# Score products of both token tiles in one block, and a fixed order for TensorE inside the token mixer

## The chip, the cores and the metric

The kernel runs on one core of a Trainium2 chip. The metric is the device time of one execution in microseconds (us), taken as the median of several runs. Besides it there is one profiled execution of the kernel before, from whose trace all durations below are read.

## The reference

The kernel computes a trunk of two layers on x of 256 tokens by 1024 channels, in float32, conditioned by a vector c. Each layer is a half-step SwiGLU feed-forward block (inner width 2816), a token mixer, and another half-step feed-forward block, each of them behind an RMS norm with shift and scale. The change is in the token mixer, which is this, cut to what matters:

```
def token_mixing(n, ...):
    proj = n @ w_in                              # qa 512, ka 128, va 128, qd 512, kd 512, vd 512 columns
    qa = axial_rope(rms_norm(qa), ...)           # 8 query heads of 64
    ka = axial_rope(rms_norm(ka), ...)           # 2 key heads of 64
    ya = gqa_attention(qa, ka, va) @ w_ba        # softmax(q k^T / 8) v, 4 query heads per key head
    od = diff_attention(qd, kd, vd, lam, slopes) # 4 heads, w = softmax(s0 + bias) - lam * softmax(s1 + bias)
    od = rms_norm(od, subln_g) * (1.0 - lam_init)
    yb = od.reshape(b, s, B_WIDTH) @ w_bb
    g = jax.nn.sigmoid(n @ w_gate + b_gate)
    ga, gb = jnp.split(g, 2, axis=-1)
    return (ga * ya + gb * yb) @ w_o
```

## The kernel before

**Products.** Every float32 matrix product is made of three products of half-split operands: high by high, low by high, high by low (`mm3`, L86 to L88). A weight comes by DMA into one of four `raw` buffers of 128x1024; ACT casts it to its high half `whi` (L328), DVE subtracts to get the low half `wlo` (L330). TensorE (PE) then streams products of 128 rows by 128x256, most of them straight after one another.

**The order of the work.** The kernel's text gives one list of steps for each layer's mixer (L1024 to L1093). A scheduler takes that list and sets the order of instructions on each engine by times that it simulates for itself, so that on PE a step of the list that would have to wait is moved behind products of a later step. What was read from PSUM comes in four general banks (`gen`, taken by turns: transposes, scores, `od`, `ont`) and four accumulating banks (`acc`).

**Branch A.** `post_kv(t)` makes the rotated and normed keys `kr` of token tile t on DVE; the norm's power is taken on POOL (L124). `to_T` transposes the queries `qr` (four transposes) and the keys `kr` (one) on PE into a `tt` bank (L787); DVE subtracts the low halves `qaT`, `kaT` (L791). Between and after these stand the projections `proj_T("qd", part)` and `proj_T("kd", part)`, 48 products each into `pt` banks. `a_scores(jj, t)` makes the scores of pair jj of query heads for one token tile: 12 products whose contraction is over 64 rows, in two `gen` banks (L840). DVE takes the maxima `nmx` (L844) and ACT the exponentials `p` (L852). `a_norm` scales them, `a_T` transposes them, `a_pv` multiplies them with the values.

**Branch B.** `b_scores(pair, t)` makes 12 products of 64 rows as well (L909), into two `gen` banks that DVE reads into `xb` (L916, adding the distance penalty and taking the maximum), ACT takes the exponentials, `b_norm` makes the difference of the two maps on DVE (L933, L934), `b_T(hd)` transposes one head, `b_out(t)` multiplies with `vd` into `od`, and `b_outT(t)` scales `od` to `on` (L970), transposes it into an `ont` bank (L973) and splits it (`onf` L977, `odL` L981).

**The gate.** `gate_mm(j, half)`, 24 full products into an `acc` bank `gt`, sixteen of them per layer, stands between these steps.

During the mixer DVE and ACT also take part in the weights of the next stage: `gacc` (L276) and `raw·cb` (L245) read a raw weight of 128x1024 on DVE. The mixer of layer 0 lies at about 205 to 345 us in the trace and that of layer 1 at about 742 to 880 us.

Of the kernel before, what the change touches and what calls it, by code (L numbers as in the profile page):

```python
# [19 lines left out]
P = 128  # L20
D = 1024
S = 256
L = 2
# [19 lines left out]
def trunk(tc, a):  # L43
    nc = tc.nc
    with (
# [38 lines left out]

        def mm3(out, Lh, Ll, Rh, Rl, start, stop):
            nc.tensor.matmul(out, Lh, Rh, start=start, stop=False, skip_group_check=True)  # L86
            nc.tensor.matmul(out, Ll, Rh, start=False, stop=False, skip_group_check=True)  # L87
            nc.tensor.matmul(out, Lh, Rl, start=False, stop=stop, skip_group_check=True)  # L88
# [26 lines left out]
        for hf in range(2):  # L115
            x = slice(hf * 512, (hf + 1) * 512)
            bank = gen("cb")
            cmm = nc.tensor.matmul(bank, ones[0:1, :], crow[hf], start=True, stop=True)
            cact = nc.scalar.activation(cb[:, x], bank, AF.Silu)
# [169 lines left out]
        def gate_bcast(l, s):  # L289
# [5 lines left out]
            for hf in range(2):  # L295
# [5 lines left out]
                nc.tensor.matmul(bank, onesr, gh, start=True, stop=False, skip_group_check=True)  # L301
                nc.tensor.matmul(bank, onesr, gl, start=False, stop=True, skip_group_check=True)
# [57 lines left out]
        class Norm:  # L360
# [37 lines left out]
            def transposes(self):  # L398
                self.banks = []
                for hf in range(2):  # L400
                    bank = gen("nt")
                    for i in range(4):
                        nc.tensor.transpose(bank[:, i * P:(i + 1) * P], self.xs[hf][:, i * P:(i + 1) * P], ident)
# [89 lines left out]
        def tok_hi(bank, ncol, unit_of, nT, t):  # L493
# [4 lines left out]
            for k in range(NK):  # L498
# [3 lines left out]
                nc.tensor.matmul(bank, nh[:, k, tok], wh[:, x], start=k == 0, stop=False, skip_group_check=True)  # L502
                nc.tensor.matmul(bank, nh[:, k, tok], wl[:, x], start=False, stop=False, skip_group_check=True)

        def tok_lo(bank, ncol, unit_of, nT, t, last):
            nh, nl = nT
            tok = slice(t * P, (t + 1) * P)
            for k in range(NK):
                u, i, c = unit_of(k)
                wh, wl = half(u, i)  # L510
                nc.tensor.matmul(bank, nl[:, k, tok], wh[:, c:c + ncol], start=False, stop=k == NK - 1, skip_group_check=True)
# [37 lines left out]
        def first_T(hts):  # L549

            tb = gen("tb")
            for t in range(2):
                for c in range(2):
                    nc.tensor.transpose(tb[:, c * 256 + t * P:c * 256 + (t + 1) * P], hts[t][:, c * P:(c + 1) * P], ident)
# [6 lines left out]
        def ffn(i, nT, norm1, first, nT_next):  # L561
# [6 lines left out]
            def down_mm(idx, t, hf, last, y=slice(0, 512), part=False):  # L568
# [4 lines left out]
                for c in range(2):  # L573
                    x = slice(c * 512 + y.start, c * 512 + y.stop)
                    if part and c == 1:

                        for L, R in ((hh, wh), (hl, wh)):
                            nc.tensor.matmul(acc[t][hf], L[:, c, tok], R[:, x], start=False, stop=False, skip_group_check=True)
                        for z in (slice(0, PART), slice(PART, 512)):
                            nc.tensor.matmul(acc[t][hf][:, z], hh[:, c, tok], wl[:, 512 + z.start:512 + z.stop], start=False,  # L580
# [136 lines left out]
        def mixer(i, nT, norm1, consts, nT_next):  # L717
# [65 lines left out]
            def to_T(src, dst, t, n):  # L783

                bank = gen("tt")
                for i in range(n):
                    nc.tensor.transpose(bank[:, i * P:(i + 1) * P], src[:, i * P:(i + 1) * P], ident)  # L787
# [44 lines left out]
            def a_scores(jj, t):  # L832
# [3 lines left out]
                for i in range(2):  # L836
                    for x, y in ((0, 0), (1, 0), (0, 1)):
                        for v in range(2):
                            pr = slice(v * 64, (v + 1) * 64)
                            nc.tensor.matmul(banks[v][:, i * 256:(i + 1) * 256], st["qaT"][x][pr, 2 * jj + i, tok], kaT[y][pr, 0, :],  # L840
# [29 lines left out]
            def a_T(jj, i):  # L870
                for v in range(2):
                    bank = gen("pt")
                    for t in range(2):
                        for c in range(2):
                            nc.tensor.transpose(bank[:, c * 256 + t * P:c * 256 + (t + 1) * P],
# [5 lines left out]
            def a_pv(jj):  # L881
                ot = gen("ot")

                for i in range(2):
                    for c in range(2):
                        for v in range(2):
                            nc.tensor.matmul(ot[v * 64:(v + 1) * 64, i * 256:(i + 1) * 256], va[:, c, v * 64:(v + 1) * 64],
# [12 lines left out]
            def b_scores(pair, t):  # L900
# [3 lines left out]
                for m in range(2):  # L904
                    ch = m * 2 + pair
                    for x, y in ((0, 0), (1, 0), (0, 1)):
                        for e in range(2):
                            pr = slice(e * 64, (e + 1) * 64)
                            nc.tensor.matmul(scs[e][:, m * 256:(m + 1) * 256], st["qdT"][x][pr, ch, tok], st["kdT"][y][pr, ch, :],  # L909
# [26 lines left out]
            def b_T(hd):  # L936
                bank = gen("wt")
                for t in range(2):
                    for c in range(2):
                        nc.tensor.transpose(bank[:, c * 256 + t * P:c * 256 + (t + 1) * P], xs[hd, t][0][:, c * P:(c + 1) * P], ident)  # L940
# [7 lines left out]
            def b_out(t):  # L948
                tok = slice(t * P, (t + 1) * P)
                od = gen("od")  # L950
                for hd in range(4):
                    for c in range(2):
                        nc.tensor.matmul(od[:, hd * P:(hd + 1) * P], wTs[hd][:, c, tok], st["vd"][:, c, hd * P:(hd + 1) * P],
# [10 lines left out]
            def b_outT(t):  # L964
# [7 lines left out]
                for hd in range(4):  # L972
                    nc.tensor.transpose(bank[:, hd * P:(hd + 1) * P], on[:, hd * P:(hd + 1) * P], ident)  # L973
# [52 lines left out]
            st["qaT"] = pair("qaT")  # L1026
            to_T(st["qr"][0], st["qaT"], 0, 4)
# [7 lines left out]
            a_scores(0, 0)  # L1035
# [370 lines left out]
```

## Time and profile before

| | |
|---|---|
| median of 3 runs | 1097.06 us (1096.51 to 1097.66) |
| profiled execution, its own time | 1097.68 us |
| its span | 1095.9 us |
| granted TensorE clock, mean | 0.999 |
| PE busy | 1082.9 us, 99% of the span, 7796 instructions |
| DVE busy | 864.9 us, 79%, 1388 instructions |
| ACT busy | 593.1 us, 54%, 916 instructions |
| POOL busy | 44.5 us, 4%, 52 instructions |
| chain that ended last | PE 94% of it, DVE 3% |

The shares are averages over the whole span. PE is nearly always at work, so a change is worth what it adds to or takes from PE's own time, or what it makes PE wait; an engine that has idle time overall can still be late at one place. The profiled execution spends 1.8 us outside the span.

### The profile page before, as it was taken

To read this page: it belongs to the slowest core of one execution; us is meant where nothing else is said; L and a number is where in the kernel's file an instruction comes from. 1 tells how busy PE (TensorE), PEld (TensorE's weight loads), DVE (VectorE), ACT (ScalarE), POOL (GpSimd) and SP (SyncE) were. 2 spreads that over 40 slices of the span, in tenths; PEclk is the share of its full clock that TensorE was granted. 3 is DMA by queue.
4 is the path that set the end of the run, shared out by engine and by line. 5 is a ranking of instruction groups with operands and counts; after the bars stand their busy time and mean duration, and the time that the engine had idled before them with its cause. 6 is when DMAs were issued, how large, how long until landed. Compare 5 with 4: busy or idle time off the path is not lost.

```text
span 1095.9 us, 19235 instructions
## 1 busy us (share of the span) xinstructions
PE 1082.9 (99%) x7796; PEld 998.8 (91%) x7796; DVE 864.9 (79%) x1388; ACT 593.1 (54%) x916; POOL 44.5 (4%) x52
## 2 busy tenths in 40 slices
PE   8999999999999999999999999999999999999997
PEld 6989999898999899999989999989889998999996
DVE  5998986899978798886589886569988779766543
ACT  5564483558664554535455545435776547444432
POOL 1000000220010000000000000004000000000000
PEclk9999999999999999999999999999999999999999
DMA  8998996368745299997449987543865454876501
GB/s 315 380 368 336 380 335 219 120 263 332 264 172 193 86 376 357 347 377 266 150 152 357 365 288 285 202 165 126 297 236 189 157 190 183 315 267 229 197 19 39
DMA packets 44889, 271.12 MB, mean 247 GB/s; under 512 B 5880, under 2 KB 6648, under 8 KB 14848
## 3 DMA queue, kind: packets, MB, share of 16 engines
q1 hardware_dynamic: 42340, 267.93, 66.1%
q10 hardware_dynamic: 2460, 1.96, 0.6%
q8 instruction: 61, 1.00, 0.3%
q14 instruction: 28, 0.23, 0.1%
HBM read 268.82 MB, written 1.05 MB: 246 GB/s over the span
## 4 chain that ended last, share of the span: by engine, by line
PE 94%; DVE 3%; ACT 1%; issue 1%; POOL 0%; POOLq 0%
PE dn L87 6%; PE dn L88 6%; PE dn L86 6%; PE u L86 6%; PE g L86 6%; PE u L87 6%; PE g L88 6%; PE g L87 6%; PE u L88 6%; PE gt L86 3%; PE gt L88 3%; PE gt L87 3%; PE g L1199 2%; PE u L1199 2%; PE yb L88 1%; PE yb L87 1%
## 5 line engine op out<-in xcount | busy, mean ns | idle before, releaser
L330 DVE TENSOR_TENSOR wlo<-raw,whi 128x1024 fp32r<-128x1024 f32 x364 | 436.9, 1220 | 133.7 <-PE u L87 44.6
L328 ACT CAST whi<-raw 128x1024 fp32r<-128x1024 f32 x364 | 374.0, 1052 | 226.4 <-PE u L88 83.7
L86 PE MATMUL u<-nh,whi 128*128 128x256 f32 x592 | 164.0, 277 | 0.0
L86 PE MATMUL g<-nh,whi 128*128 128x256 f32 x592 | 164.0, 277 | 0.0
L87 PE MATMUL u<-nh,wlo 128*128 128x256 f32 x592 | 163.7, 277 | 0.0
L88 PE MATMUL g<-nl,whi 128*128 128x256 f32 x592 | 163.7, 277 | 0.0
L87 PE MATMUL g<-nh,wlo 128*128 128x256 f32 x592 | 163.7, 277 | 0.0
L88 PE MATMUL u<-nl,whi 128*128 128x256 f32 x592 | 163.6, 276 | 0.0
L86 PE MATMUL dn<-whi,hh 128*128 128x512 f32 (+1 forms) x326 | 126.0, 387 | 0.0
L87 PE MATMUL dn<-whi,hl 128*128 128x512 f32 (+1 forms) x326 | 125.9, 386 | 0.0
L88 PE MATMUL dn<-wlo,hh 128*128 128x512 f32 (+1 forms) x326 | 125.8, 386 | 0.0
L86 PEld LDWEIGHTS g<-nh,whi 128*128 128x128 f32 x592 | 111.2, 188 | 0.3
L87 PEld LDWEIGHTS g<-nh,wlo 128*128 128x128 f32 x592 | 111.2, 188 | 0.2
L86 PEld LDWEIGHTS u<-nh,whi 128*128 128x128 f32 x592 | 111.2, 188 | 0.1
L87 PEld LDWEIGHTS u<-nh,wlo 128*128 128x128 f32 x592 | 111.3, 188 | 0.0
L88 PEld LDWEIGHTS u<-nl,whi 128*128 128x128 f32 x592 | 111.2, 188 | 0.2
L88 PEld LDWEIGHTS g<-nl,whi 128*128 128x128 f32 x592 | 111.2, 188 | 0.0
L245 DVE CUSTOM_DVE_ANT_0 raw<-raw,cb 128x1024 f32<-128x1024 f32 x80 | 95.5, 1217 | 1.1 <-DMA raw<-in_ada_t_dram 0.9
L86 PE MATMUL gt<-nh,whi 128*128 128x256 f32 x256 | 73.7, 288 | 0.0
L88 PEld LDWEIGHTS dn<-wlo,hh 128*128 128x128 f32 x326 | 61.2, 188 | 12.4
L87 PEld LDWEIGHTS dn<-whi,hl 128*128 128x128 f32 x326 | 61.3, 188 | 11.1 <-DVE hl L546 0.2
L86 PEld LDWEIGHTS dn<-whi,hh 128*128 128x128 f32 x326 | 61.3, 188 | 11.1
(227 smaller groups left out, 2051.9 us busy)
## 6 DMA issues: line engine op xcount, KB each, us to landing
raw<-in_w_gu_dram SPq DMA_DIRECT2D x79, 1024.0 KB, 5.5
raw<-in_w_d_dram SPq DMA_DIRECT2D x41, 1024.0 KB, 6.4
raw<-in_ada_t_dram SPq DMA_DIRECT2D x40, 1024.0 KB, 6.8
raw<-in_ada_g_dram SPq DMA_DIRECT2D x24, 1024.0 KB, 6.3
raw<-in_w_in_dram SPq DMA_DIRECT2D x16, 1024.0 KB, 5.0
raw<-in_w_gate_dram SPq DMA_DIRECT2D x16, 1024.0 KB, 4.9
raw<-in_ada_t_dram SPq DMA_DIRECT2D x16, 512.0 KB, 6.5
raw<-in_w_gu_dram SPq DMA_DIRECT2D x32, 256.0 KB, 6.1
```

Source lines behind the costliest of these rows:

```text
L86: nc.tensor.matmul(out, Lh, Rh, start=start, stop=False, skip_group_check=True)
L87: nc.tensor.matmul(out, Ll, Rh, start=False, stop=False, skip_group_check=True)
L88: nc.tensor.matmul(out, Lh, Rl, start=False, stop=stop, skip_group_check=True)
L245: queue("dve", nc.vector.tensor_tensor_reduce(r, r, cb, 1.0, 0.0, op0=ALU.mult, op1=ALU.add, accum_out=col[:, k:k + 1]))
L328: split[1] = nc.scalar.copy(hi, r)
L330: split[0] = nc.vector.tensor_tensor(lo, r, hi.bitcast(F32), op=ALU.subtract)
L1199: nc.tensor.matmul(bank[:, c * 256:(c + 1) * 256], W[:, w], N[:, k, :], start=x + y + k + c == 0, stop=y == 1 and k == NK - 1, skip_group_ ...
```

## The change

A small class `Ordered` wraps PE's `matmul` and `transpose`. While its flag `on` is set, every PE instruction is tied behind the one issued before it (an order on the same engine, no semaphore). The flag is set from the first `to_T` of the mixer to its last `gate_mm`, in each layer. So the scheduler can no longer move PE's instructions against one another there: what the list says is what PE does, and a PE instruction that isn't ready holds all that stand behind it. The list itself is written anew: the score steps of both token tiles stand together (`a_scores(0,0)`, `a_scores(0,1)`, and so on), and so do `a_T`, `b_T` and `b_outT` of a pair.

```diff
+        class Ordered:
+            on, last = False, None
+            def then(self, ins):
+                if self.on and self.last is not None:
+                    follow(ins, self.last)
+                self.last = ins
+                return ins
+            def matmul(self, *args, **kw):
+                return self.then(nc.tensor.matmul(*args, **kw))
+            def transpose(self, *args, **kw):
+                return self.then(nc.tensor.transpose(*args, **kw))
+        pe = Ordered()
         def mm3(out, Lh, Ll, Rh, Rl, start, stop):
-            nc.tensor.matmul(out, Lh, Rh, start=start, stop=False, skip_group_check=True)
+            pe.matmul(out, Lh, Rh, start=start, stop=False, skip_group_check=True)
...
             st["qaT"] = pair("qaT")
+            pe.on = True
             to_T(st["qr"][0], st["qaT"], 0, 4)
             to_T(st["kr"][0], kaT, 0, 1)
             qd, kd = [], []
             proj_T("qd", 0, qd)
             post_kv(1, kv[1])
             to_T(st["qr"][1], st["qaT"], 1, 4)
             to_T(st["kr"][1], kaT, 1, 1)
             proj_T("qd", 1, qd)
             a_scores(0, 0)
+            a_scores(0, 1)
             proj_T("kd", 0, kd)
             a_norm(0, 0)
-            a_scores(0, 1)
+            a_norm(0, 1)
             proj_T("kd", 1, kd)
-            a_norm(0, 1)
             a_T(0, 0)
+            a_T(0, 1)
             vd0 = proj("vd", 0)
-            a_T(0, 1)
             st["vd"] = slot("vd", (P, 2, 512))
             nc.scalar.copy(st["vd"][:, 0, :], vd0)
+            a_pv(0)
+            vd1 = proj("vd", 1)
+            nc.scalar.copy(st["vd"][:, 1, :], vd1)
             a_scores(1, 0)
-            vd1 = proj("vd", 1)
-            a_norm(1, 0)
-            a_pv(0)
-            nc.scalar.copy(st["vd"][:, 1, :], vd1)
             a_scores(1, 1)
...
             gate_mm(2, 1)
+            b_scores(0, 0)
+            b_scores(0, 1)
+            gate_mm(3, 0)
+            b_norm(0, 0)
             b_norm(0, 1)
+            gate_mm(3, 1)
             b_scores(1, 0)
-            gate_mm(3, 0)
-            b_T(0)
-            gate_mm(3, 1)
-            b_T(1)
-            b_norm(1, 0)
             b_scores(1, 1)
             free(4)
             cap_w[0] = CAP2
             gate_mm(4, 0)
+            b_T(0)
+            b_T(1)
             gate_mm(4, 1)
+            b_norm(1, 0)
             b_norm(1, 1)
             gate_mm(5, 0)
+            gate_mm(5, 1)
             b_T(2)
-            gate_mm(5, 1)
             b_T(3)
+            gate_mm(6, 0)
             b_out(0)
-            gate_mm(6, 0)
             b_out(1)
             free(3)
             gate_mm(6, 1)
+            gate_mm(7, 0)
             b_outT(0)
-            gate_mm(7, 0)
             b_outT(1)
             gate_mm(7, 1)
+            pe.on = False
             gate_bcast(l, 1)
```

Nothing is added to or taken from any engine's instructions; only their order, and with it their waits, differ. In the changed file the helper lines stand 9 to 21 lines further down, and all products carry L97, all transposes L100.

On PE, at the start of the ordered part in layer 0, this stood before: `tt` is the bank of the transposes, `pt_2536` and `pt_2537` are banks of `proj_T("qd", …)`, and `kr_2466` are the keys of token tile 0.

```order
L787 MATMUL tt_2525<-ident,qr_2407 128x128 x4
L86 MATMUL pt_2536<-nh_164,whi_2299 128x256
L87 MATMUL pt_2536<-nh_164,wlo_2300 128x256
...
L86 MATMUL pt_2537<-nh_164,whi_2431 128x256
L87 MATMUL pt_2537<-nh_164,wlo_2432 128x256
L787 MATMUL tt_2532<-ident,kr_2466 128x128
L88 MATMUL pt_2537<-nl_165,whi_2431 128x256
```

In the changed kernel the same place, and the one for token tile 1 (`qr_2519`, `kr_2614`), reads:

```order
L97 MATMUL kv_2469<-whi_2256,nl_165 128x256 x4
L100 MATMUL tt_2525<-ident,qr_2407 128x128 x4
L100 MATMUL tt_2532<-ident,kr_2466 128x128
L97 MATMUL pt_2536<-nh_164,whi_2299 128x256
...
L97 MATMUL pt_2537<-nl_165,whi_2431 128x256
L100 MATMUL tt_2617<-ident,qr_2519 128x128 x4
L100 MATMUL tt_2624<-ident,kr_2614 128x128
L97 MATMUL pt_2536<-nh_164,whi_2441 128x256
```

The transpose of the keys of tile 0 stood 35 products behind that of the queries and now stands right behind it; for tile 1 it stood 36 products behind and now stands right behind too.

On DVE, around the keys of token tile 1 in layer 0, before:

```order
L779 TENSOR_TENSOR q_432_2609<-kv_2469,ropes_1727 128x4x16 x2
L791 TENSOR_TENSOR qaT_2524<-tt_2617,qaT_2523 128x4x128
L820 TENSOR_TENSOR q_431_2607<-q_431_2607,q_432_2609 128x128
L276 SCALAR_TENSOR_TENSOR gacc_2115<-raw_2495,ccol,gacc_2115 128x1024
L825 TENSOR_SCALAR kr_2614<-q_431_2607,hr_2605 128x64 x2
L276 SCALAR_TENSOR_TENSOR gacc_2115<-raw_2495,ccol,gacc_2115 128x1024
L791 TENSOR_TENSOR kaT_2306<-tt_2624,kaT_2305 128x128
```

And after:

```order
L798 TENSOR_TENSOR q_432_2609<-kv_2469,ropes_1727 128x4x16 x2
L295 SCALAR_TENSOR_TENSOR gacc_2115<-raw_2495,ccol,gacc_2115 128x1024
L839 TENSOR_TENSOR q_431_2607<-q_431_2607,q_432_2609 128x128
L295 SCALAR_TENSOR_TENSOR gacc_2115<-raw_2495,ccol,gacc_2115 128x1024
L844 TENSOR_SCALAR kr_2614<-q_431_2607,hr_2605 128x64 x2
L810 TENSOR_TENSOR qaT_2524<-tt_2617,qaT_2523 128x4x128
L810 TENSOR_TENSOR kaT_2306<-tt_2624,kaT_2305 128x128
```

Between the last part of the rotation (`q_432`) and the keys there stood one `qaT` and one `gacc`; now two `gacc` stand there and `qaT` comes behind the keys.

On PE, at the end of the mixer in layer 0, the two transposes of `b_outT` (`ont`) stood with 24 products of a gate between them before:

```order
L88 MATMUL gt_3772<-nl_165,whi_3534 128x256
L973 MATMUL ont_3855<-ident,on_3850 128x128 x4
L86 MATMUL gt_3866<-nh_164,whi_3624 128x256
...
L88 MATMUL gt_3866<-nl_165,whi_3624 128x256
L973 MATMUL ont_3902<-ident,on_3897 128x128 x4
L86 MATMUL gt_3866<-nh_164,whi_3652 128x256
```

And after:

```order
L97 MATMUL gt_3850<-nl_165,whi_3599 128x256
L97 MATMUL gt_3850<-nh_164,whi_3599 128x256
L97 MATMUL gt_3850<-nh_164,wlo_3600 128x256
L97 MATMUL gt_3850<-nl_165,whi_3599 128x256
L100 MATMUL ont_3886<-ident,on_3881 128x128 x4
L100 MATMUL ont_3902<-ident,on_3897 128x128 x4
L97 MATMUL gt_3850<-nh_164,whi_3640 128x256
```

The second group of four now follows the first with nothing in between, and the 24 products stand ahead of both.

## Rows read from the trace of the kernel before

**Rows 1.** PE's waits, 736 to 880 us: waiting instruction, releaser, total us, times, longest.
```profile
PE pt L875 <- ACT p L864: 0.2, 1, 0.2
```

**Rows 2.** PE timeline around one score block: start us, us, instruction, count.
```profile
269.68 0.28 PE L88 MATMUL gt<-nl,whi 128*128 128x256 f32 x1
269.88 0.98 PE L909 MATMUL scb<-kd,qd 64*128 64x256 f32 x12
270.79 0.38 PE L86 MATMUL gt<-nh,whi 128*128 128x256 f32 x1
271.02 0.28 PE L87 MATMUL gt<-nh,wlo 128*128 128x256 f32 x1
```

**Rows 3.** PE timeline, the first and last stretch of score products in layer 0.
```profile
233.88 0.50 PE L840 MATMUL sc<-kaT,qaT 64*128 64x256 f32 x4
...
294.54 0.98 PE L909 MATMUL scb<-kd,qd 64*128 64x256 f32 x12
```

**Rows 4.** PE timeline around the transposes of queries and keys, layer 0.
```profile
219.98 0.60 PE L787 MATMUL tt<-ident,qr 128*128 128x128 f32 x4
220.33 0.37 PE L86 MATMUL pt<-nh,whi 128*128 128x256 f32 x1
...
224.40 0.27 PE L787 MATMUL tt<-ident,kr 128*128 128x128 f32 x1
```

**Rows 5.** DVE timeline around both keys, layer 0.
```profile
223.71 0.42 DVE L825 TENSOR_SCALAR kr<-q,hr 128x64 f32<-128x64 f32 x2 [0.63 <-POOL hr L124]
...
231.02 1.28 DVE L276 SCALAR_TENSOR_TENSOR gacc<-raw,ccol,gacc 128x1024 f32<-128x1024 f32 x1
232.21 0.41 DVE L825 TENSOR_SCALAR kr<-q,hr 128x64 f32<-128x64 f32 x2
```

**Rows 6.** POOL timeline, the two powers behind these keys.
```profile
220.55 3.13 POOL L124 TENSOR_TENSOR hr<-hms,mhalf 128x2 f32<-128x2 f32 x1
...
230.24 0.73 POOL L124 TENSOR_TENSOR hr<-hms,mhalf 128x2 f32<-128x2 f32 x1
```

**Rows 7.** PE timeline behind the queries' transposes of tile 0, layer 1.
```profile
757.02 0.37 PE L86 MATMUL pt<-nh,whi 128*128 128x256 f32 x1
```

**Rows 8.** DVE timeline, both keys of layer 1.
```profile
758.76 0.41 DVE L825 TENSOR_SCALAR kr<-q,hr 128x64 f32<-128x64 f32 x2
...
768.35 0.41 DVE L825 TENSOR_SCALAR kr<-q,hr 128x64 f32<-128x64 f32 x2
```

**Rows 9.** DVE timeline behind the keys of tile 1, layer 0.
```profile
234.02 2.35 DVE L330 TENSOR_TENSOR wlo<-raw,whi 128x1024 fp32r<-128x1024 f32 x2
236.28 1.28 DVE L750 TENSOR_TENSOR qd<-pt,qd 128x512 fp32r<-128x512 f32 x2
237.48 0.68 DVE L844 TENSOR_REDUCE nmx<-sc 128x2 f32<-128x512 f32 x1
```

**Rows 10.** ACT by line and shape, 210 to 345 us: busy us, mean ns | idle before.
```profile
L852 ACT ACTIVATE p<-sc,bi,qsc 128x256 f32<-128x256 f32 x16 | 8.9, 561 | 3.9 <-DVE bi L847 3.2 <-PE pt L88 0.6
```

**Rows 11.** DVE timeline in the gate stage of layer 0.
```profile
276.02 0.42 DVE L916 CUSTOM_DVE_ANT_0 xb<-scb,pen 128x256 f32<-128x256 f32 x1
...
276.37 1.22 DVE L245 CUSTOM_DVE_ANT_0 raw<-raw,cb 128x1024 f32<-128x1024 f32 x1
...
280.54 0.61 DVE L933 TENSOR_SCALAR xb<-xb,c 128x256 f32<-128x256 f32 x2
281.07 0.87 DVE L934 SCALAR_TENSOR_TENSOR xb<-xb,rs 128x256 f32<-128x256 f32 x2
```

**Rows 12.** DVE timeline around the two `b_outT` of layer 0.
```profile
317.42 0.75 DVE L977 TENSOR_SCALAR onf<-ont,subg 128x512 f32<-128x512 f32 x1 [1.05 <-PE ont L973]
...
319.52 0.35 DVE L970 TENSOR_SCALAR on<-od,or 128x128 f32<-128x128 f32 x1
```

**Rows 13.** Stretches at the end: us, busy of PE, PEld, DVE, ACT, POOL, granted clock, DMA.
```profile
1090.00:1094.00 4.00, 0.00 (x0) 0.00 (x0) 1.76 (x4) 1.15 (x3) 0.86 (x1) 1.00 0.23 87
1094.00:1096.00 2.00, 0.00 (x0) 0.00 (x0) 0.00 (x0) 0.00 (x0) 0.00 (x0) 0.50 0.23 88
```

More of the change, by code (lines that the diff above doesn't have):

```diff
@@ L117, in trunk @@
             bank = gen("cb")
-            cmm = nc.tensor.matmul(bank, ones[0:1, :], crow[hf], start=True, stop=True)
+            cmm = pe.matmul(bank, ones[0:1, :], crow[hf], start=True, stop=True)
             cact = nc.scalar.activation(cb[:, x], bank, AF.Silu)
@@ L402, in transposes @@
                     for i in range(4):
-                        nc.tensor.transpose(bank[:, i * P:(i + 1) * P], self.xs[hf][:, i * P:(i + 1) * P], ident)
+                        pe.transpose(bank[:, i * P:(i + 1) * P], self.xs[hf][:, i * P:(i + 1) * P], ident)
                     self.banks.append(bank)
@@ L786, in to_T @@
                 for i in range(n):
-                    nc.tensor.transpose(bank[:, i * P:(i + 1) * P], src[:, i * P:(i + 1) * P], ident)
+                    pe.transpose(bank[:, i * P:(i + 1) * P], src[:, i * P:(i + 1) * P], ident)
                 tok = slice(t * P, (t + 1) * P)
@@ L839, in a_scores @@
                             pr = slice(v * 64, (v + 1) * 64)
-                            nc.tensor.matmul(banks[v][:, i * 256:(i + 1) * 256], st["qaT"][x][pr, 2 * jj + i, tok], kaT[y][pr, 0, :],
+                            pe.matmul(banks[v][:, i * 256:(i + 1) * 256], st["qaT"][x][pr, 2 * jj + i, tok], kaT[y][pr, 0, :],
                                              start=x + y == 0, stop=y == 1, skip_group_check=True)
@@ L874, in a_T @@
                         for c in range(2):
-                            nc.tensor.transpose(bank[:, c * 256 + t * P:c * 256 + (t + 1) * P],
+                            pe.transpose(bank[:, c * 256 + t * P:c * 256 + (t + 1) * P],
                                                 probs[jj, v, t][:, i * 256 + c * P:i * 256 + (c + 1) * P], ident)
@@ L939, in b_T @@
                     for c in range(2):
-                        nc.tensor.transpose(bank[:, c * 256 + t * P:c * 256 + (t + 1) * P], xs[hd, t][0][:, c * P:(c + 1) * P], ident)
+                        pe.transpose(bank[:, c * 256 + t * P:c * 256 + (t + 1) * P], xs[hd, t][0][:, c * P:(c + 1) * P], ident)
                 if hd % 2 == 0:
@@ L972, in b_outT @@
                 for hd in range(4):
-                    nc.tensor.transpose(bank[:, hd * P:(hd + 1) * P], on[:, hd * P:(hd + 1) * P], ident)
+                    pe.transpose(bank[:, hd * P:(hd + 1) * P], on[:, hd * P:(hd + 1) * P], ident)
                 if t == 0:
@@ L1263, in keep_busy @@
             for _ in range(n):
-                ins = nc.tensor.matmul(bank.rearrange("p (r x) -> p r x", r=4), ident, ident4, start=True, stop=True)
+                ins = pe.matmul(bank.rearrange("p (r x) -> p r x", r=4), ident, ident4, start=True, stop=True)
                 follow(ins, first_)
@@ L1289, in turn @@
             for i in range(4):
[L1290 removed]
+                tr = pe.transpose(nts[t, hf][:, i * P:(i + 1) * P], xs[:, i * P:(i + 1) * P], ident)
             return tr
```

35 lines of the change are left out of this document (16 added, 19 removed).

## The prediction

> **What bounds the kernel now.** I read the page first: PE is busy nearly all of the span (99%, in the table above), so only PE's own work and PE's waits count. Then I read PE's waits in each mixer. In layer 1 there is a single one, of 0.2 us [rows 1]; in layer 0 the list names none behind the start of the ordered part either. The reader should see two things in that. There is no wait that this change could remove. And the transposes, which depend on DVE and ACT, cost no wait only because the scheduler placed each behind products that were ready: the transpose of the keys starts at 224.40, 4.1 us behind the one of the queries, with 35 products between them [rows 4]. Third, I read PE's timeline at the score blocks for what a block costs, and DVE's at the same places for when each operand is ready.
>
> **What is saved.** A full product takes 0.116 us: (224.40 − 220.33) / 35 [rows 4]. A score product takes (0.98 − 0.50) / 8 = 0.06 [rows 2, 3]. A block also has a price of its own. Twelve products hold 269.88 to 270.79, 0.91 us, which is 0.19 more than 12 × 0.06. The last full product ahead stands for 0.20 (269.68 to 269.88), 0.09 more than its neighbours, and the first behind for 0.23 (270.79 to 271.02), 0.11 more [rows 2]. That is 0.39 per block. The order before has the products of layer 0 in 11 stretches (some of the eight blocks are split) and those of layer 1 in 9 (the first and the last of layer 0 stand in [rows 3]); the order of the change has 4 in each. So 12 blocks × 0.39 = 4.7 us. Some 19 groups of transposes and `od` products also come to stand beside another group; by the exit alone that is 0.09 each, 1.7 us. **Saved: 6.4 us.** Bounds: 4.7 if the groups of transposes save nothing, 7.3 if three products that stood unpaired in layer 0 gain too.
>
> **What is added.** In the ordered part a PE instruction that isn't ready holds everything behind it, and what is behind it are full products that could have run. I go through the places in order, for each taking when PE would arrive and when the operand is there.
>
> *1. Keys of tile 0.* The transpose now stands right behind that of the queries, so PE arrives at 220.33 [rows 4]. DVE writes the keys from 223.71 to 224.13, and what it waited for was the power on POOL, which took 3.13 us from 220.55 [rows 5, 6]. Wait 3.8 us. Layer 1: PE arrives at 757.02 [rows 7], keys at 758.76 + 0.41 [rows 8], wait 2.15.
>
> *2. Keys of tile 1.* From 224.1 PE does the transpose (0.2), 48 products (5.6) and the queries' transposes (0.35, 219.98 to 220.33 [rows 4]), and arrives at 230.25. Before, the keys were written by 232.62. DVE now has a second `gacc` (1.19, 231.02 to 232.21 [rows 5]) ahead of them in place of a `qaT` (0.6, as for the like subtraction `qd`: half of 236.28 to 237.48 [rows 9]), so 233.2: wait 3.0. The bounds are 2.4, if DVE's order did not matter, and 3.6. The upper one is for the power on POOL, which starts at 230.24 and takes 0.73 alone, while the one before took 3.13 [rows 6]: if the `gacc` that now comes first holds it up, the keys come 0.6 later. The Trainium skill ("SBUF — State Buffer", section "SBUF: two separate sides") says that a DVE instruction with two SBUF inputs and a GpSimd instruction that reads SBUF exclude each other for a whole instruction. By that rule this wait would be 3.6 and the whole forecast 0.6 longer; the power of 3.13 us, during which DVE worked on a `wlo`, agrees with it. I keep 3.0, because that `gacc` may also start late enough. Layer 1: PE arrives at 759.2 + 6.1 = 765.3, keys at 768.76 [rows 8], wait 3.5.
>
> *3. a_T(0).* Between the keys of tile 1 and these transposes PE has 48 products of `qd`, the block of 24 (1.6 + 0.2) and 96 products of `kd`: 18.6 us. DVE has, in its new order up to the last `bi`: `qaT` and `kaT` 0.8, six `wlo` at 1.13 (half of 234.02 to 236.28 [rows 9]) 6.8, two `gacc` 2.4, four `raw·cb` of about 1.15 4.6 (its 1.22 less the overlap that consecutive rows show, as 236.28 + 1.28 against 237.48), two `qd` 1.2, four `nmx` of 0.6 2.4, small ones 0.3: 18.5. Then ACT still has two exponentials of 0.56 [rows 10] and about as much again to scale them, 2.1. So 20.6 against 18.6: wait 2.0; for layer 1, where DVE starts later by the wait in 2 but PE does too, I take 1.5. Bounds 0 (DVE's 18.5 alone is hidden) and 3.
>
> *4. Banks of branch B.* There are four `gen` banks. The block of pair 0 fills all four, the block of pair 1 needs all four read, and `b_T(0)`, `b_T(1)` need two banks of pair 1 read. From the first read of pair 0 to the fourth bank and then two of pair 1, DVE has in its new order 12 reads into `xb` at 0.35 (276.02 to 276.37 [rows 11]) 4.1, three `wlo` 3.4, two `raw·cb` 2.3, four each of L933 and L934 (0.27 and 0.40 [rows 11]) 2.7, and fourteen small ones 1.0: 13.5, and some 0.5 for ACT's exponentials between them: 14.0. PE has 48 products of the gate (5.5), the block (1.8), 24 more products (2.7) and 0.4 at the edges: 10.4. Wait 3.6, in each layer. Bounds 1.5 (two of the `wlo` fall behind) and 4.5.
>
> *5. b_T(2), b_T(3).* PE has 72 products and four transposes, 8.8; DVE four reads 1.4, four `wlo` 4.5, the norms 2.7 and 1.0 small, 9.6, and ACT's eight exponentials of about 0.56 stand partly between (up to 2.3 of their 4.5). Wait 0.8 to 3.1; I take 3.0, since each norm needs both of its exponentials and cannot be started ahead.
>
> *6. b_outT.* The second four transposes now follow the first four. Before, DVE did `onf` from 317.42, when the first transposes were done, and the last `on` was written at 319.52 + 0.35 = 319.87 [rows 12]: 2.45 later, hidden by 24 products. Now those 24 stand ahead, so it is open. I take 2.3 (the last of the row is partly overlap).
>
> Layer 0: 3.8 + 3.0 + 2.0 + 3.6 + 3.0 + 2.3 = 17.7. Layer 1: 2.15 + 3.5 + 1.5 + 3.6 + 3.0 + 2.3 = 16.05; for places 4 to 6 I use layer 0's rows for both, as the order is the same. **Added: 33.8 us.**
>
> Nothing is lost elsewhere: weights and DMAs only get ahead while PE waits. Net 33.8 − 6.4 = +27.4. On the profiled 1097.68 that is 1125.1, whose own time lies 0.6 above the median; on the median 1097.06 it is 1124.5. I say **1125 us**.
>
> **The rivals.**
>
> *The waits are not there, and only the blocks count.* If the operands were early enough for the new order, the 6.4 saved remain: 1090.7 us, faster by 0.6%. For it: the waits of before are nearly none [rows 1]. Against it: that is because of the order that is taken away, and the transposes of the keys cannot start ahead of 224.13. This decides if the six waits sum to less than 6.4 in both layers; place 1 and 2 alone hold 12.45. Chance 0.04.
>
> *Only the waits for the keys remain.* The 3 us in which PE stands let DVE and ACT get ahead, and places 3 to 6 are then hidden: 3.8 + 3.0 + 2.15 + 3.5 = 12.45, less 6.4, +6: 1103 us. For it: the table of the profile shows ACT and DVE idle for a part of the span. Against it: DVE's rows behind the keys follow one another without a gap [rows 9], so it doesn't get ahead within the mixer, and places 4 and 6 come from the order, not from the load. Chance 0.15.
>
> *The clock falls.* Several of the waits are 3 us or more. If the granted clock drops to its lower level in four of them, and products take twice their 0.116 us for some 4 to 8 us afterwards, that adds 2 to 4 us each, 8 to 16: 1133 to 1141, say 1137. Against it: at the end of the kernel PE has no work in 1090 to 1094, and the granted clock is still 1.00 there; it is 0.50 in the next stretch [rows 13], so it took an idle time longer than any wait foreseen here. The Trainium skill ("TensorE: Matmul & The Clock Gate", section "Why this matters for your kernels") advises against idle gaps between bursts of matmuls, since the clock then goes back down. It would speak against this change, and the rows bear it out only for a longer gap than these. Chance 0.10.
>
> **How the numbers follow.** My forecast has 0.71. Its own range by the bounds: low 1125 − (2.0 + 1.5 in place 3, 4.2 in place 4, 4.4 in place 5, 1.2 in place 2), not all at once, about 1114; high about 1132. The range for 8 in 10 reaches to part of the neighbours, 1109 to 1136. What a measurement here can tell from no change is about 0.2%, 2.2 us. Faster has the first rival, 0.04; no change would need waits of about 6.4 us, 0.02; slower has the rest, 0.94.
>
> **What would show each step.** In the profile after, PE's waits should name the transposes of the keys behind `kr` (some 3 to 4 us each, four in all), `a_T` behind ACT's `p`, score products of pair 1 and transposes of branch B behind `xb`, and the transposes of `od` behind `on`, sum near 34. The stretches of score products should be four a layer, each of 24 in about 1.6 us. PE's busy time should hardly change. The granted clock should stay at its mean of 0.999. I would be wrong if the waits behind `kr` were under 1 us, which would mean that POOL's power came much earlier, or if the clock showed a lower level in the mixers.

## The result and the profile after

The changed kernel takes 1133.47 us (median of 4 runs, 1131.83 to 1138.49); the kernel before, in the same runs, 1097.36. The ratio is 1.0337, with a 95% interval of 1.0303 to 1.037: slower by 36 us. The forecast was 1125 us, slower by 28, in a range of 1109 to 1136. The time lies in the range, 8.5 us above the value. It lies as well inside the 1133 to 1141 that the rival of the falling clock gave, 3.5 below its 1137.

The page's first part of the changed kernel: busy time, share of the span, instructions.

```profile
PE 1094.4 (97%) x7796; PEld 1008.1 (89%) x7796; DVE 865.5 (76%) x1388; ACT 592.9 (52%) x916; POOL 45.7 (4%) x52
```

The counts are those of before; DVE and ACT have the same work. PE is idle 37.8 of its span of 1132.2 us, where it was idle 13.0 of 1095.9, and it is busy 11.5 us longer with the same instructions. The first is waits; the second goes with a clock that fell. The mean granted clock is 0.986 after 0.999 (0.984 to 0.990 in the four executions). All of it lies inside the ordered part: from the first transpose of the queries to the end of the gate's broadcast, the two mixers take 120.79 and 123.67 us in place of 104.28 and 102.96, 37.2 us more, and the rest of the span is 0.9 us shorter.

PE's waits in the changed kernel, 200 to 370 us and then 750 to 915 us (waiting instruction, releaser, total, times, longest):

```profile
PE tt L100 <- DVE kr L844: 4.1, 2, 3.7
PE pt L100 <- ACT p L883: 2.7, 2, 2.3
PE wt L100 <- DVE xb L953: 2.6, 2, 1.5
PE ont L100 <- DVE on L989: 1.7, 2, 1.2
PE wt L100 <- DVE mx L935: 1.6, 2, 1.1
...
PE scb L97 <- DVE mx L935: 0.9, 1, 0.9
```

```profile
PE tt L100 <- DVE msh L269: 3.2, 1, 3.2
PE wt L100 <- DVE xb L953: 2.2, 2, 1.1
PE tt L100 <- DVE kr L844: 1.9, 1, 1.9
PE ont L100 <- DVE on L989: 1.7, 2, 1.2
PE scb L97 <- DVE mx L935: 1.5, 1, 1.5
PE pt L100 <- ACT p L883: 0.4, 1, 0.4
```

These are the six places of the prediction, and no others: the keys (`tt`; the release by `msh` L269 is an instruction of DVE right behind the keys), `a_T` (`pt`), the banks of branch B (`scb`, and `wt` behind `mx`), `b_T(2)` and `b_T(3)` (`wt` behind `xb`) and the transposes of `od` (`ont`). Their sum is 24.5 us, in 19 waits: 13.6 in layer 0 and 11.0 in layer 1.

PE's timeline at the keys of both tiles of layer 0, which answers to [rows 4]:

```profile
219.11 0.60 PE L100 MATMUL tt<-ident,qr 128*128 128x128 f32 x4
223.41 0.48 PE L100 MATMUL tt<-ident,kr 128*128 128x128 f32 x1 [3.70 <-DVE kr L844]
...
231.64 0.60 PE L100 MATMUL tt<-ident,qr 128*128 128x128 f32 x4
232.59 0.30 PE L100 MATMUL tt<-ident,kr 128*128 128x128 f32 x1 [0.35 <-DVE kr L844]
```

The first wait is as foreseen, 3.70 for 3.8. The second is 0.35 where 3.0 was foreseen, and the reason is in the granted clock (the third number from the end of a row) of the stretches between:

```profile
220.00:224.00 4.00, 0.59 (x3) 0.59 (x4) 3.37 (x7) 3.03 (x6) 2.90 (x1) 0.77 0.88 326
224.00:228.00 4.00, 4.00 (x21) 4.00 (x21) 4.00 (x8) 1.36 (x3) 2.84 (x3) 0.50 0.64 256
228.00:232.00 4.00, 4.00 (x33) 4.00 (x32) 4.00 (x8) 0.27 (x1) 2.27 (x2) 0.87 0.54 152
```

Behind the wait the clock is at its lower level, 0.50 or 1.2 GHz, and PE does 21 products in 4 us where it does 38 at the full clock (the rows of the filled kernel below). From the keys of tile 0 to those of tile 1 it needs 8.8 us (223.41 to 232.24) where 6.1 were reckoned, and the keys have caught up. In stretches of 2 us over both mixers the lower level adds up to 30.7 us in the changed kernel, behind seven of the waits, and to nothing in the kernel before.

The block of 24 products in the changed kernel, which answers to [rows 2]:

```profile
238.09 0.28 PE L97 MATMUL pt<-nl,whi 128*128 128x256 f32 x1
238.29 1.63 PE L97 MATMUL sc<-kaT,qaT 64*128 64x256 f32 x24
239.85 0.38 PE L97 MATMUL pt<-nh,whi 128*128 128x256 f32 x1
240.07 0.28 PE L97 MATMUL pt<-nh,wlo 128*128 128x256 f32 x1
```

It holds PE for 1.56 us, where two blocks of 12 hold it for 1.82 and 0.20 more at their extra pair of edges. So this pair saves 0.46 us. The first block of layer 1 takes 1.56 as well; the others of 24 that don't wait take 1.61 to 1.62, which saves 0.40. The forecast was 0.39.

### The profile page after: what moved, and what is told of

Read it like the earlier page. It is cut to its first block, busy times and chain, and to the rows that moved or that the text cites. A ratio compares the mean times of both kernels' runs of the same rounds, so it can differ in the third digit from the quotient of the medians.

```text
span 1132.2 us, 19246 instructions
## 1 busy us (share of the span) xinstructions
PE 1094.4 (97%) x7796; PEld 1008.1 (89%) x7796; DVE 865.5 (76%) x1388; ACT 592.9 (52%) x916; POOL 45.7 (4%) x52
## 3 DMA queue, kind: packets, MB, share of 16 engines
q10 hardware_dynamic: 2460, 1.96, 0.6%
## 4 chain that ended last, share of the span: by engine, by line
PE 83%; DVE 10%; ACT 3%; issue 3%; DMA 1%; POOL 1%; POOLq 0%; DVEq 0%; ACTq 0%
PE dn L97 20%; PE g L97 20%; PE u L97 20%; PE gt L97 5%; PE yb L97 4%; PE wo L97 4%; DVE wlo L349 3%; PE gu L97 3%; PE pt L97 2%; PE pj L97 2%; DVE raw L264 1%; DMA raw<-in_ada_t_dram 1%; DVE nf L445 1%; PE nt L100 1%; PE od L97 1%
## 5 line engine op out<-in xcount | busy, mean ns | idle before, releaser
L97 PE MATMUL g<-nh,whi 128*128 128x256 f32 x656 | 179.9, 278 | 1.1 <-ACT nh L1234 0.6
L97 PE MATMUL g<-nh,wlo 128*128 128x256 f32 x656 | 179.4, 277 | 0.1
L97 PE MATMUL u<-nh,whi 128*128 128x256 f32 x656 | 179.5, 277 | 0.0
L97 PE MATMUL u<-nh,wlo 128*128 128x256 f32 x656 | 179.2, 277 | 0.0
L97 PE MATMUL g<-nl,whi 128*128 128x256 f32 x656 | 179.1, 277 | 0.0
L97 PE MATMUL u<-nl,whi 128*128 128x256 f32 x656 | 179.1, 277 | 0.0
L97 PE MATMUL dn<-whi,hh 128*128 128x512 f32 (+1 forms) x358 | 138.5, 387 | 0.0
L97 PE MATMUL dn<-wlo,hh 128*128 128x512 f32 (+3 forms) x390 | 138.5, 368 | 0.0
L97 PE MATMUL dn<-whi,hl 128*128 128x512 f32 (+1 forms) x358 | 138.4, 387 | 0.0
L97 PEld LDWEIGHTS g<-nh,whi 128*128 128x128 f32 x656 | 123.2, 188 | 2.8 <-ACT whi L347 1.3
L97 PEld LDWEIGHTS g<-nh,wlo 128*128 128x128 f32 x656 | 123.4, 188 | 0.7 <-DVE wlo L349 0.5
L97 PEld LDWEIGHTS u<-nh,wlo 128*128 128x128 f32 x656 | 123.5, 188 | 0.0
L97 PEld LDWEIGHTS u<-nl,whi 128*128 128x128 f32 x656 | 123.2, 188 | 0.2
L97 PEld LDWEIGHTS g<-nl,whi 128*128 128x128 f32 x656 | 123.2, 188 | 0.0
L97 PEld LDWEIGHTS u<-nh,whi 128*128 128x128 f32 x656 | 123.2, 188 | 0.0
L97 PEld LDWEIGHTS dn<-wlo,hh 128*128 128x128 f32 x390 | 73.2, 188 | 14.9
L97 PEld LDWEIGHTS dn<-whi,hl 128*128 128x128 f32 x358 | 67.3, 188 | 12.4 <-DVE hl L565 0.3
L97 PEld LDWEIGHTS dn<-whi,hh 128*128 128x128 f32 x358 | 67.3, 188 | 12.3
L97 PE MATMUL gt<-nh,whi 128*128 128x256 f32 x256 | 76.4, 299 | 0.0
```

Source lines behind the costliest of these rows:

```text
L97: return self.then(nc.tensor.matmul(*args, **kw))
```

## The experiments

Theory A is that of the prediction: the fixed order makes each wait, and each has its own chain. Rival B: the grouping makes the waits, whatever orders PE. Rival C: waits at the keys come back later, since another engine is the limit. Theory D was formed after the first four runs: in the mixer DVE is nearly as full as PE, so that what comes to DVE late makes PE late.

**The new list without the fixed order.**

```diff
-            pe.on = True
+            pe.on = False
```

> The new list, but the flag is never set, so the scheduler may move TensorE's instructions as before. Theory A (the fixed order makes the waits, the clock falls behind some of them): the waits of the mixers, 22.7 us in the changed kernel, go, the clock stays at 1.00, and what is left is the saving of fewer blocks: 1090 to 1094 us. Rival B (the grouping itself makes waits, since four banks and the softmax chain are too short for blocks of both tiles): most of the 36 us stays, over 1110 us.

1113.78 us, ratio 1.0144 (1.0128 to 1.016). The time lies in rival B's range, but less than half of the 36 us stays, not most: the list alone costs 16.6, and fixing its order the other 20. (The waits put at 22.7 us there are the 24.5 above.) PE's waits in this kernel, 207 to 345 us:

```profile
PE gb L97 <- DVE gl L319: 2.6, 1, 2.6
PE wt L100 <- DVE mx L935: 1.6, 1, 1.6
PE pt L100 <- ACT p L883: 1.3, 1, 1.3
```

The scheduler did move the keys' transposes back behind products. A new wait stands at the gate's broadcast (`gb`), 2.6 us in either layer: the list puts both `b_outT` at its very end, and `gl` on DVE comes behind their work and a `wlo`. The clock is at its lower level for 10.2 us behind waits of the two mixers.

**The old list with the fixed order.** The list of before, with the flag set at the same place.

> The list of before, with the flag set over the same part. Theory A: the transposes of both keys wait as in the changed kernel (9.2 us in both layers, and a fall of the clock behind the long ones), and no block is saved: 1110 to 1125 us. Rival B: without the grouping nothing waits: 1095 to 1100 us.

1119.05 us, ratio 1.0201 (1.0182 to 1.0219), as theory A said. The same 3.70 for the keys in layer 0, 1.95 and 3.44 in layer 1, and 3.1 at `a_T` in either. So fixing the order costs 22 us without any grouping, 15.6 of them as waits; the lower level stands at 17.1 us.

**The fixed order from the first score block on.**

```diff
-            pe.on = True
             to_T(st["qr"][0], st["qaT"], 0, 4)
...
             proj_T("qd", 1, qd)
+            pe.on = True
             a_scores(0, 0)
```

> The changed kernel, but the flag is set only behind the second projection of qd, so the transposes of queries and keys may move; the scheduler puts those of the keys of tile 1 behind all products of qd, with the first block right behind them. Theory A: the four waits for keys (9.2 us) and the falls of the clock behind them (13.8 us at the lower level, of which 1 to 2 while PE waits, so some 6 us of lost work) go; 1 to 2 us in each layer stand in front of the first block instead, and the transposes of a_T may wait 1 to 4 us more: 1119 to 1126 us. If the falls of the clock cost nothing: 1126 to 1130 us. Rival C (the waits for keys are made up later, since DVE and ACT get ahead in them): no change, 1131 to 1135 us.

1129.19 us, ratio 1.0289 (1.027 to 1.0309): 4.3 us less than the changed kernel, where theory A wanted 7 or more; it lies in the range for falls of the clock that cost nothing. The first rows of PE's waits, 207 to 345 us:

```profile
PE pt L100 <- ACT p L883: 4.8, 3, 3.5
PE wt L100 <- DVE xb L953: 2.6, 2, 1.5
```

The waits for the keys shrink to 0.6 in layer 0 and to nothing in layer 1, but `a_T` now waits 4.8 behind ACT where it waited 2.7. Over both layers 9.2 us at the keys become 0.6, while 2.0 are new at the first score block and `a_T` goes from 3.0 to 7.3; all waits together go from 24.5 to 22.6 and the lower level from 30.7 to 23.9. Rival C holds for most of it: what PE doesn't wait at the keys it waits behind DVE's and ACT's next work.

**The two `b_outT` apart.**

```diff
             gate_mm(6, 1)
-            gate_mm(7, 0)
             b_outT(0)
+            gate_mm(7, 0)
             b_outT(1)
```

> The changed kernel, with 24 products of the gate between the two b_outT again, as before. The waits of 1.74 us in each layer go, and so do the falls of the clock behind them (3.4 us at the lower level in each layer). Theory A: 3.5 of waits and about 3 of clock, 1126 to 1128 us. If the clock's falls there have another cause than these waits: 1129 to 1131 us.

1129.52 us, ratio 1.0284 (1.0266 to 1.0301), 4.0 us less than the changed kernel: the 3.5 of waits and little else, the time that was expected if the falls there had another cause than these waits. But the falls behind `ont` are gone; there are others, and the lower level adds up to 34.1 us. Behind `a_T` of layer 0, where the changed kernel waits 2.3 us, this one waits 2.46. The stretches of this kernel and then of the changed one:

```profile
252.00:256.00 4.00, 2.64 (x11) 2.24 (x12) 2.60 (x10) 4.00 (x12) 0.00 (x0) 0.60 1.00 416
256.00:260.00 4.00, 4.00 (x15) 3.38 (x14) 2.47 (x5) 1.50 (x3) 0.00 (x0) 0.54 0.24 61
```

```profile
252.00:256.00 4.00, 2.31 (x18) 2.04 (x19) 2.60 (x10) 4.00 (x12) 0.00 (x0) 1.00 1.01 403
256.00:260.00 4.00, 4.00 (x19) 3.30 (x18) 2.55 (x5) 1.37 (x3) 0.00 (x0) 1.00 0.23 72
```

Nearly the same wait is followed by a fall in one kernel and by none in the other. A fall belongs to waits, but not to one wait for certain.

**The waits filled with products of no use.** A helper puts products into the bank that is filled next.

```diff
+            def fill(bank, n):
+                for _ in range(n):
+                    pe.matmul(bank[:, 0:256], nh[:, 0, 0:P], nh[:, 0, :], start=True, stop=True, skip_group_check=True)
...
                 bank = gen("tt")
+                if n == 1:
+                    fill(bank, ((30, 15), (22, 26))[t][l])
...
                     bank = gen("pt")
+                    if (jj, i, v) == (0, 0, 0):
+                        fill(bank, (18, 3)[l])
...
                 bank = gen("wt")
+                if hd > 1:
+                    fill(bank, (12, 9)[l] if hd == 2 else 9)
...
                 bank = gen("ont")
+                if t == 1:
+                    fill(bank, 9)
```

> The changed kernel with products of no use (0.116 us each, into the bank that is filled next) in front of the transposes that wait longest: 30 and 15 ahead of the keys of tile 0 in layers 0 and 1, 22 and 26 ahead of those of tile 1, 18 and 3 ahead of a_T, 12, 9 and 9, 9 ahead of b_T(2), b_T(3), 9 ahead of the second transposes of b_outT. They fill most of a wait and should lengthen nothing, but TensorE is not idle. If the idle time is what makes the clock fall, the granted clock stays at 1.00 at these places. Then the time tells what the falls cost in all: 1119 to 1122 us if the half of their 30.7 us is lost in full, 1127 to 1130 us if most of it comes back because TensorE arrives later at its next wait. If the clock has another cause: falls as in the changed kernel, 1132 to 1136 us.

1129.9 us, ratio 1.0297 (1.0278 to 1.0316). The stretches of 220 to 232 us in this kernel:

```profile
220.00:224.00 4.00, 3.88 (x33) 3.68 (x32) 3.37 (x8) 3.13 (x5) 3.13 (x2) 1.00 0.98 354
224.00:228.00 4.00, 4.00 (x38) 4.00 (x36) 4.00 (x9) 1.50 (x3) 2.84 (x3) 1.00 0.63 250
228.00:232.00 4.00, 4.00 (x37) 4.00 (x36) 3.98 (x10) 0.75 (x2) 2.27 (x2) 1.00 0.39 123
```

Its PE timeline behind the products of qd:

```profile
229.36 0.60 PE L100 MATMUL tt<-ident,qr 128*128 128x128 f32 x4
229.72 2.88 PE L97 MATMUL tt<-nh 128*128 128x256 f32 x22
232.44 0.27 PE L100 MATMUL tt<-ident,kr 128*128 128x128 f32 x1
```

DVE's row of the keys of tile 1 there:

```profile
231.86 0.42 DVE L850 TENSOR_SCALAR kr<-q,hr 128x64 f32<-128x64 f32 x2
```

Where PE is kept at work the clock stays at 1.00, and PE reaches the queries of tile 1 at 229.36, not at 231.64; the 22 filling products, 2.72 us of PE's time, then stand where the keys are not ready yet (DVE writes them by 231.86 + 0.42 = 232.28). The lower level falls from 30.7 us to 10.2, and what is left stands behind the waits for banks, which were not filled. So idle time is what lowers the clock. But the time falls by 3.6 us only, not by the 10 that half of 20.5 would be: PE arrives earlier at its next wait and waits longer. The fillers hold PE for 22.7 us in all and 7.5 us of waits are left, together 30.2 where the changed kernel waits 24.5.

**Less work for DVE in the changed kernel.** The modulation's products run over 64 of 1024 elements, so the rest of the modulation is left out.

```diff
-            queue("dve", nc.vector.tensor_tensor_reduce(r, r, cb, 1.0, 0.0, op0=ALU.mult, op1=ALU.add,
+            z = slice(0, 64)
+            queue("dve", nc.vector.tensor_tensor_reduce(r[:, z], r[:, z], cb[:, z], 1.0, 0.0, op0=ALU.mult, op1=ALU.add,
                                                         accum_out=col[:, k:k + 1]))
```

> The changed kernel, with the modulation's products of the conditioning on DVE (30 in the two mixers, 1.15 us each) cut to 64 of 1024 elements, so the modulation is computed from a part of c only. DVE has some 32 us less to do in the two mixers. Theory D (in the mixer DVE is nearly as full as TensorE, so what it has to do there is what it is late by): half or more of the change's loss goes, 1110 to 1118 us. Theory A alone (each wait is the latency of one chain behind a fixed order): 1124 to 1131 us, as only the places behind such a product gain.

1115.11 us, ratio 1.0156 (1.0133 to 1.018): 18.4 us less, half of the loss, as theory D said. The two mixers of the kernel before (busy times of PE, PEld, DVE, ACT, POOL), and then those of this one:

```profile
219.98:324.26 104.28, 104.22 (x858) 96.86 (x857) 97.92 (x230) 73.17 (x153) 10.21 (x11) 1.00 0.71 263
756.66:859.62 102.96, 102.72 (x858) 95.68 (x857) 91.59 (x217) 72.66 (x152) 8.33 (x9) 1.00 0.64 232
```

```profile
221.43:335.76 114.33, 104.36 (x858) 97.67 (x857) 86.54 (x230) 72.44 (x153) 10.72 (x11) 0.97 0.66 244
768.21:878.35 110.14, 102.14 (x858) 95.24 (x857) 79.55 (x217) 72.17 (x152) 8.39 (x9) 1.00 0.61 221
```

In the kernel before DVE is busy for 94% of layer 0's mixer and 89% of layer 1's. In the changed kernel the same work is 83% and 74% of longer mixers (99.98 and 92.10 us): there DVE is idle too, but late at the places that count. With the load cut, `a_T`, the score blocks and `b_T(2)`, `b_T(3)` wait for nothing any more. What stays is the waits for the keys (3.61, 2.96, 1.96, 1.82), three of `b_T(0)`, `b_T(1)` for banks and those of `ont`, 18.0 us in all: these are waits that the load doesn't explain. The cut takes 26 us from DVE in the two mixers, less than the 32 expected. It also changes the times by which the scheduler plans, and DVE's order with them, while PE's stays: how much is the smaller load and how much another order on DVE is not told apart.

**Less work for DVE in the new list without the fixed order.** The same cut on the first experiment.

> The new list with the flag never set, and the same cut of DVE's work. Theory D: the loss of this list (16.6 us) came from DVE being full, so more than half of it goes: 1098 to 1107 us. Rival B (grouping makes waits for banks and chains that no engine's load explains): 1109 to 1114 us.

1106.47 us, ratio 1.0075 (1.0054 to 1.0096). It gains 7.3 of the 16.6 us, a little under the half that theory D asked, and some 2 of these 7.3 the kernel before gains as well (next run). Left are two waits a layer, 1.67 at `b_T` for a bank and 2.59 at the gate's broadcast, and 10.2 us of lower clock: the list's own chains at its end.

**Less work for DVE in the kernel before.** The control.

> The kernel before with the same cut of DVE's work, as the control for the two others. TensorE hardly waits there, so all theories expect 0 to 2 us of gain: 1095 to 1097 us.

1095.72 us, ratio 0.9983 (0.9973 to 0.9992): about 2 us less, since PE didn't wait there.

**Only the pairing.** The flag is never set; the blocks are paired, and the rest stands as in the list of before.

```diff
             a_scores(0, 0)
+            a_scores(0, 1)
             proj_T("kd", 0, kd)
             a_norm(0, 0)
-            a_scores(0, 1)
...
             vd1 = proj("vd", 1)
...
+            a_scores(1, 0)
             a_scores(1, 1)
...
             b_scores(0, 0)
+            b_scores(0, 1)
             gate_mm(1, 0)
...
             b_scores(1, 0)
+            b_scores(1, 1)
             gate_mm(3, 0)
             b_T(0)
             gate_mm(3, 1)
             b_T(1)
```

> Only the pairing: the flag is never set, the score steps of both token tiles stand together in the list, but the transposes, b_out and b_outT stand between gate steps as in the kernel before, and pair 0 of branch B comes as early as there. The scheduler still splits some blocks: 9 and 6 stretches of score products in the two layers in place of 11 and 9, worth 5 x 0.39 = 2 us. Theory D (DVE is nearly full in the mixer, and a paired block gives it its work later and all at once): waits of 3 to 6 us take that and more, 1098 to 1103 us. If the saving of a block can be had: 1094 to 1096 us.

1105.61 us, ratio 1.0073 (1.0058 to 1.0088), slower than either theory expected, though theory D's sign is right. The waits listed are only 2.5 us. PE's timeline at a stretch that the scheduler cut off a block of branch B:

```profile
269.21 0.28 PE L97 MATMUL gt<-nh,whi 128*128 128x256 f32 x1
270.07 0.97 PE L97 MATMUL scb<-kd,qd 64*128 64x256 f32 x6 [0.59 <-ACT p L871]
270.97 0.38 PE L97 MATMUL gt<-nh,wlo 128*128 128x256 f32 x1
```

The scheduler issues the six products of one bank by themselves; that it does so because banks come free one by one is argued, not tested. Six of one half take 0.90 us, as long as twelve that alternate between two banks and two halves of the rows (0.91 in [rows 2]). In layer 0 the products of branch B take 6.12 us from start to start, where they take 3.64 in the kernel before. And the clock fell once here, behind a single wait of 1.09 us in layer 1 (PE's timeline, then a stretch):

```profile
810.14 0.98 PE L97 MATMUL scb<-kd,qd 64*128 64x256 f32 x6 [1.09 <-ACT p L871]
```

```profile
812.00:814.00 2.00, 2.00 (x9) 1.78 (x9) 1.93 (x12) 2.00 (x7) 0.00 (x0) 0.50 0.73 307
```

The lower level lasts 6.8 us, worth up to 3.4 of the 8 us lost.

**Only the first pair.** The list of before with the first two score steps together, the flag not set.

> The kernel before with one step moved: the first two score steps of branch A stand together, and the flag is not set. 10 and 8 stretches in place of 11 and 9. Theory D: no difference, 1096.5 to 1098 us, since DVE is busy at that place. If the saving of a block can be had: 0.8 us less, 1096 us, which this measurement would hardly show.

1097.22 us, ratio 1.0000 (0.999 to 1.0009): no difference, with 9 and 8 stretches of score products.

**The pairing with less work for DVE.**

> The list of the pairing alone with the cut of DVE's work of the earlier control (the modulation is computed from a part of c). Theory D: with room on DVE the waits of the pairing go and the saving shows: 1093 to 1097 us, at or below the control's 1095.7. Rival B (banks and chains, whatever the load): 1099 to 1103 us.

1094.74 us, ratio 0.9973 (0.9963 to 0.9982), 1.0 us under the control, whose interval it overlaps. With this cut the pairing costs nothing: all blocks but the first of a layer stay whole (5 stretches a layer, 9 in the control) and PE waits 0.4 us a layer. Eight stretches less at 0.39 would be 3.1, less these waits; what is seen of it is about 1 us, at the edge of what can be measured.

## Why the prediction came out as it did

**What bounds the kernel.** Right that the kernel before has no wait to remove and that the scheduler's moves were what hid the transposes. Incomplete: the mixers have a second bound beside PE, DVE with 94% and 89%. The prediction saw that DVE's rows follow one another without a gap [rows 9] and used that only against a rival. About half of the loss goes when DVE's work is cut. No kernel with the full work on DVE was faster than the one before; that DVE's load is the reason is likely, and not shown, as the pairing with the cut gained only some 1 us on its control.

**What is saved.** The sum of 6.4 us took 0.39 per block; a merged pair saves 0.40 to 0.46. The saving exists on PE and is lost among the waits. Of the 1.7 us for groups of transposes the sum below shows nothing.

**What is added, place by place** (layers 0 and 1). Keys of tile 0: 3.70 and 1.95 for 3.8 and 2.15. Keys of tile 1: 0.35 and 3.16 for 3.0 and 3.5. `a_T`: 2.68 and 0.36 for 2.0 and 1.5. Banks of branch B: 2.47 and 1.51 for 3.6. `b_T(2)`, `b_T(3)`: 2.64 and 2.25 for 3.0. `b_outT`: 1.73 in each for 2.3. Sum 24.5 for 33.8. The mechanism was right at all six places; two terms are far off, the keys of tile 1 in layer 0 and the banks in layer 1 (1.51 for 3.6); `a_T` in layer 1 and the banks in layer 0 are 1.1 short. Ahead of the first the clock is at its lower level, so PE comes later; the second has a fall at the end of its first wait (853.65 to 860.48 us), and no further wait behind that. That the slow clock is what shortened the later wait is shown for the keys: with the wait before filled and the clock kept, the keys came 2.56 us behind PE (229.72 to 232.28), where the wait had been 0.35 and the forecast 3.0. For the banks it is only argued. The prediction gave a wait behind `kr` of under 1 us as a sign of being wrong, by an earlier power on POOL; one came, by a slower PE.

**The clock.** This is the step that failed: "it took an idle time longer than any wait foreseen here", read from the end of the kernel [rows 13]. The sum had the clock at nothing, and the two signs set for that failed: the clock showed its lower level in the mixers, and PE's busy time grew by 11.5 us. The clock stayed at 1.00 at the end for 5.0 us behind the last product (1088.96 to 1093.98), and yet in the mixers it fell behind waits of 1.1 to 3.7 us, at other places in each kernel. One end of one kernel was no bound: in the kernel with only the first pair together, the level falls 2.0 us behind the last product (1088.43 to 1090.45). The rule that the prediction set beside it (the Trainium skill, "TensorE: Matmul & The Clock Gate", section "Why this matters for your kernels", against idle gaps between bursts) agrees with these runs: 30.7 us at the lower level, and 1.00 where the gaps were filled. Some of the falls came behind shorter gaps than the page names, and there the measurement decides. The rival's 8 to 16 us are near what the falls cost by themselves, some 14 (below); what it had wrong was to put them on top of all waits: the falls also take waits away, and taking two thirds of them out gave back 3.6 us.

**The sum.** Of the 37.2 us in the two mixers, 24.5 are waits as the profile lists them. The rest is estimated. Each of the 19 waits adds the tail of a product that nothing overlaps (0.28 less 0.116, together 3.1). Of the 30.7 us at the lower level 28.9 lie outside the waits, and half of that, 14.4, is lost. That is 42.0, and a saving of 4.8 closes it, for the 6.4 of the forecast. In the forecast's own terms, from PE's arrival to the operand, a tail belongs to its wait: 27.6 for 33.8. In the filled kernel, whose clock fell less, fillers, waits and tails come to 32.2. So the waits were sized nearly right for a full clock, and the value of 1125 was too low mostly because the clock was left out. That the time still lies in the range is in part luck: the falls cost some 14 us that the sum had at nothing, and took some 5 from the waits.

**POOL's lock.** The prediction left open whether the `gacc` that now comes first holds up the power on POOL. It probably does, but for nothing: the power's row on POOL, and on DVE those of two `gacc` and of the keys, in the changed kernel:

```profile
229.47 2.04 POOL L143 TENSOR_TENSOR hr<-hms,mhalf 128x2 f32<-128x2 f32 x1
```

```profile
229.45 1.28 DVE L295 SCALAR_TENSOR_TENSOR gacc<-raw,ccol,gacc 128x1024 f32<-128x1024 f32 x1
...
230.84 1.28 DVE L295 SCALAR_TENSOR_TENSOR gacc<-raw,ccol,gacc 128x1024 f32<-128x1024 f32 x1
232.04 0.41 DVE L844 TENSOR_SCALAR kr<-q,hr 128x64 f32<-128x64 f32 x2
```

The power takes 2.04 us, 0.73 before [rows 6], and ends at 231.51, 0.78 behind the end of the first `gacc` (230.73). So far this agrees with the Trainium skill ("SBUF — State Buffer", section "SBUF: two separate sides"). The second `gacc`, which by that rule could not run beside the power, doesn't agree: it starts at 230.84 and takes its usual 1.28 while the power still runs, though spans on POOL are rough. DVE is ready for the keys only at 232.04, so the 0.6 us was rightly left out of the sum, but not for the reason given: the first `gacc` did not start late enough; the second one kept DVE busy.

**The rivals.** That only the waits of the keys remain was tested from its other side: taking these away gave 4.3 us, not 9 and more, since 6.3 of the 9.2 us came back at the first score block and at `a_T`. That the waits are not there and 6.4 us are won is out, with DVE as it is.

What stays open: why a wait of 2.32 us keeps the clock in one kernel and 2.46 us loses it in another, and how the 18 us that the light DVE gave split between shorter waits and fewer falls (the lower level went from 30.7 us to 6.8 there), and how much of them is DVE's changed order.

## What to carry to other kernels

Where a scheduler hides a transpose behind ready products, an order fixed by hand has to give each step the lead that it had; count for each instruction when PE arrives and when the operand is there, before fixing. Before merging small blocks on PE, look at the busy share of the engine that reads them in that stage, not in the whole span: DVE was busy 79% overall and 94% where the change was made, and there a saving on PE bought nothing. And a wait on PE can cost more than its length, as the clock may fall behind it.

## What the runs showed of the hardware

- The granted clock fell to 0.50, for 3.4 or 6.8 us at a time in the mixers, behind single waits as short as 1.09 us (810 us of the kernel with only the pairing) and 1.51 us (854 us of the changed kernel), while the 4 us without work at the end of the kernel before still show 1.00 [rows 13].
- Twelve score products of 64 rows that alternate between two halves took 0.91 us; six of one half alone took 0.90.
- The small power on POOL took 0.73, 2.04 or 3.13 us, with other work of DVE beside it each time.
